# Hybrid attention block: x of the second half scaled by its token norm once, on arrival, and the products with rbc and rcol left out

## Chip, cores and metric

One core of a Trainium2 chip. The metric is the device time of one execution in microseconds, the median of several runs. Engines: TensorE (PE, with its weight loads PEld), VectorE (DVE), ScalarE (ACT), GpSimd (POOL); SyncE (SP) issues most transfers.

## What is computed

A decoder block on x of 1024 tokens by 1024 features: an RMS norm, one projection into eleven parts, latent attention with 8 heads (MLA), gated linear attention with 4 heads (GLA), gates, an output projection, the residual and a final norm. Cut to what matters here:

```python
h = rmsnorm(x, g_in)                       # x * rsqrt(mean(x*x) + EPS) * g_in
proj = h @ w_in
(c_q, c_kv, k_r, z_mla, q_g, k_g, v_g, a_lr, z_gla, gate_mla, gate_gla) = split(proj)
q  = rmsnorm(c_q, g_q) @ w_uq              # latent attention: queries
kv = rmsnorm(c_kv, g_kv) @ w_ukv           # keys and values
y_mla = (mla_attention(q, k, v) * silu(z_mla)) @ w_proj_mla
log_a = log_sigmoid(a_lr @ w_gla_gate + b_gla_gate) / 16
y_gla = (rmsnorm(gla_chunked(q_g, k_g, v_g, log_a), g_gla) * silu(z_gla)) @ w_proj_gla
merged = sigmoid(gate_mla) * y_mla + sigmoid(gate_gla) * y_gla
out = rmsnorm(x + merged @ w_out, g_final)
```

The norm's factor is one number per token (r below). Since it multiplies a whole row of x, it may be applied to x or to each product x @ w.

## The kernel before

The tokens are worked in two halves of 512, h = 0 and h = 1, one after the other. Activations lie transposed, features on partitions and the 512 tokens along the row. Each fp32 product is made of three: both operands are split into a rounded high part and a low part (`split`, line 209: ACT copies to the high part, DVE or POOL subtracts for the low part), and `mm3` (line 191, matmuls at line 201) adds high x high, high x low and low x high in PSUM. Weights are fetched by SP (`load_raw`), split by ACT (`whi`, line 187) and DVE or POOL (`wlo`, line 188).

The work is a list of units per half (`units_of`): misc, the latents ckv and cq, per GLA head q, k, v and two z units, 16 gate units g, then the attention's units (uqr, uv, hi, zm), yg, ym and the output units wo. A `Stream` steps through them in order, a few matmuls at a time, and fills the waits of the side chains (`st.ride`, `tick`). A scheduler then orders each engine's instructions; every engine works its own list strictly in that order.

`prologue(h)` (line 266) fetches x for a half: four tiles transposed (`xs`, two k tiles of 128 features each), scaled by g_in alone and split into xh and xl (lines 281, 282), and four tiles by rows (`xr`), whose squares ACT sums (line 289) to ssq; `rsqrt_cols` makes rcol, r with tokens on partitions, 128 x 4. `bcast_row` (line 254) later spreads it over the partitions: four small matmuls (line 257) and a copy by ACT (line 259) give rbc, 128 x 512. For h = 1 the prologue runs among the output units of half 0 (`pro`, at the end), in pools with 3 buffers.

So x @ w still lacks r, and every user of a projection puts it in: `silu2` and the gate units multiply by rbc on DVE (lines 337, 349) ahead of ACT's tanh; the q units multiply both decay factors ep (DVE, 373) and en (POOL, 374); the values are scaled by rcol while they are split (409, 410); krr = misc x rbc (663); `latent` carries rcol in its row sums (f1, f2, f3). The 16 gate results go through DRAM (`gtd`) and are fetched again into `zr` at the end of the half; the linear branch's results come back the same way in `linear_inputs` (`ugd`), before whose last fetch all gate units must be done (line 988).

## Time and profile before

| | |
|---|---|
| median of 3 runs | 1083.74 us (1082.48 to 1083.81) |
| profiled execution | 1085.81 us, of which the span from first to last instruction is 1084.0 |
| PE busy | 1048.3 us, 97% of the span |
| DVE busy | 714.0 us, 66% |
| ACT busy | 542.1 us, 50% |
| POOL busy | 374.9 us, 35% |
| mean granted clock of PE | 0.98 |
| half 1 begins on PE | 517.81 us |

Times in the trace count from the first instruction. A row of a timeline gives start, duration, engine, line, operation, output <- inputs, shapes and count, and in brackets how long the engine had been idle and what ended that. Matmuls overlap, so a row's duration is longer than the step from one to the next. The chain of waits is followed back from the last instruction, at each step to whatever released it.

### The profile page before, as it was taken

What the parts mean: (1) busy time and instruction counts of PE and PEld (TensorE: products, weight loads), DVE (VectorE), ACT (ScalarE), POOL (GpSimd) and SP (SyncE); (2) the same over time, 40 slices, a digit from 0 to 9 for tenths busy, and PEclk for the clock granted to TensorE, in tenths of its full rate; (3) what the DMA queues carried; (4) which work ended last, traced back from release to release, by engine and by line L of the source; (5) the groups of instructions that cost most, each with busy time, mean ns of one, the idle gap of its engine ahead of it and who ended that gap; (6) DMA issues with size and microseconds to landing.
All of it is one profiled execution on the core that took longest, in us unless ns stands there. A gap on an engine that the chain in (4) does not pass through costs nothing.

```text
span 1084.0 us, 14078 instructions
## 1 busy us (share of the span) xinstructions
PE 1048.3 (97%) x5231; PEld 872.4 (80%) x5231; DVE 714.0 (66%) x1114; ACT 542.1 (50%) x910; POOL 374.9 (35%) x274
## 2 busy tenths in 40 slices
PE   8999999999999989999999999999999998999997
PEld 5798998987778867888889989988777776788875
DVE  5796555557586776466887655455767877667673
ACT  5744334455556653444574444344664656553232
POOL 2361121114445542230524211104454656533420
PEclk8899999999999999999999999999999999899999
DMA  8213213235433446644412233235422223424532
GB/s 297 98 59 97 97 60 117 97 100 195 139 98 111 144 139 250 226 138 144 165 60 78 78 102 101 80 112 158 122 96 70 81 83 121 125 90 161 175 111 98
DMA packets 46118, 132.05 MB, mean 122 GB/s; under 512 B 5232, under 2 KB 7664, under 8 KB 45920
## 3 DMA queue, kind: packets, MB, share of 16 engines
q1 hardware_dynamic: 37760, 113.96, 32.1%
q0 software_dynamic: 3680, 8.78, 3.0%
q10 hardware_dynamic: 4608, 8.39, 2.1%
q8 instruction: 41, 0.67, 0.3%
q14 instruction: 29, 0.24, 0.1%
HBM read 110.01 MB, written 21.10 MB: 121 GB/s over the span
## 4 chain that ended last, share of the span: by engine, by line
PE 77%; DVE 12%; ACT 4%; issue 2%; DMA 2%; POOL 1%; SPq 0%; POOLq 0%; DVEq 0%; ACTq 0%
PE pj L201 58%; DVE pl L943 2%; PE y L548 2%; PE y L546 2%; PE y L547 2%; PE ops L201 2%; DVE mx L893 1%; PE sc L930 1%; PE sc L932 1%; PE sc L933 1%; PE ov L951 1%; PE ov L952 1%; PE sc L886 1%; PE at L201 1%; DVE wlo L188 1%
## 5 line engine op out<-in xcount | busy, mean ns | idle before, releaser
L201 PE MATMUL pj<-xl,whi 128*128 128x512 f32 x800 | 301.0, 399 | 1.4 <-DVE xl L282 1.4
L201 PE MATMUL pj<-xh,whi 128*128 128x512 f32 x672 | 270.5, 403 | 2.4 <-ACT whi L187 1.6
L187 ACT CAST whi<-wraw 128x1024 fp32r<-128x1024 f32 (+1 forms) x151 | 155.3, 1029 | 122.0 <-PE pj L201 91.3
L201 PEld LDWEIGHTS pj<-xl,whi 128*128 128x128 f32 x800 | 153.5, 192 | 31.9 <-DVE xl L282 2.9
L201 PE MATMUL pj<-xh,wlo 128*128 128x512 f32 x672 | 176.6, 397 | 0.0
L188 POOL TENSOR_TENSOR wlo<-wraw,whi 128x1024 fp32r<-128x1024 f32 (+2 forms) x52 | 118.2, 2274 | 140.8 <-ACT whi L187 67.4
L201 PEld LDWEIGHTS pj<-xh,whi 128*128 128x128 f32 x672 | 129.7, 193 | 28.0 <-ACT whi L187 1.9
L201 PEld LDWEIGHTS pj<-xh,wlo 128*128 128x128 f32 x672 | 127.2, 191 | 26.3
L188 DVE TENSOR_TENSOR wlo<-wraw,whi 128x1024 fp32r<-128x1024 f32 x100 | 127.4, 1275 | 21.5 <-ACT whi L187 21.3
L945 POOL TENSOR_TENSOR acc<-acc,p 128x512 f32<-128x512 f32 (+3 forms) x80 | 84.9, 1061 | 86.0 <-ACT p L939 70.5
L943 DVE TENSOR_TENSOR pl<-p,ph 128x512 fp32r<-128x512 f32 (+3 forms) x80 | 70.3, 886 | 23.4 <-ACT ph L942 23.2
L939 ACT ACTIVATE p<-sc 128x512 f32<-128x512 f32 (+3 forms) x80 | 37.3, 468 | 68.8 <-DVE sc L935 50.8
L201 PE MATMUL pj<-wlo,xh 128*128 128x256 f32 x256 | 64.4, 285 | 0.0
L201 PE MATMUL pj<-whi,xh 128*128 128x256 f32 x256 | 64.2, 284 | 0.0
L893 DVE TENSOR_REDUCE mx<-sc 128x1 f32<-128x512 f32 (+2 forms) x96 | 51.8, 551 | 11.6 <-PE sc L886 10.4
L548 PE MATMUL y<-whi,zl 128*128 128x512 f32 x128 | 50.5, 396 | 0.5 <-DVE zl L211 0.5
L547 PE MATMUL y<-wlo,zh 128*128 128x512 f32 x128 | 50.4, 395 | 0.0
L546 PE MATMUL y<-whi,zh 128*128 128x512 f32 x128 | 49.5, 396 | 0.0
L201 PEld LDWEIGHTS pj<-wlo,xh 128*128 128x128 f32 x256 | 49.0, 191 | 0.3
L201 PEld LDWEIGHTS pj<-whi,xh 128*128 128x128 f32 x256 | 48.9, 191 | 0.3
L211 POOL TENSOR_TENSOR ql<-qi,qh 128x512 fp32r<-128x512 f32 x8 | 12.4, 1554 | 93.5 <-ACT qh L210 93.5
L349 DVE TENSOR_TENSOR zr<-pj,rbc 128x512 f32<-128x512 f32 x32 | 22.0, 688 | 33.8 <-PE pj L201 33.5
(298 smaller groups left out, 2101.6 us busy)
## 6 DMA issues: line engine op xcount, KB each, us to landing
wraw<-in_dram SPq DMA_DIRECT2D x141, 512.0 KB, 3.5
gtd<-zr ACTq DMA_DIRECT2D x32, 256.0 KB, 2.2
zr<-gtd SPq DMA_DIRECT2D x32, 256.0 KB, 2.9
xr<-in_dram SPq DMA_DIRECT2D x8, 512.0 KB, 9.4
ugd<-uo SPq DMA_DIRECT2D x16, 256.0 KB, 2.2
zr<-ugd SPq DMA_DIRECT2D x16, 256.0 KB, 3.1
xo<-in_dram SPq DMA_DIRECT2D x8, 512.0 KB, 5.8
xs<-in_dram SPq DMA_DIRECT2D x7, 512.0 KB, 8.6
```

The costliest lines, as they stand in the source:

```text
L187: nc.scalar.copy(out=hi[:, 0:n], in_=raw[:, 0:n])
L188: getattr(nc, lo_engine).tensor_tensor(out=lo[:, 0:n], in0=raw[:, 0:n], in1=R(hi[:, 0:n]), op=ALU.subtract)
L201: nc.tensor.matmul(out=ps, lhsT=a, rhs=b, start=(i == 0), stop=(i == 3 * n - 1))
L211: (lo_engine or nc.vector).tensor_tensor(out=lo, in0=src, in1=R(hi), op=ALU.subtract)
L349: nc.vector.tensor_tensor(out=zr, in0=c.ps, in1=c.rbc, op=ALU.mult)
L546: nc.tensor.matmul(out=c.ops[t], lhsT=a[0], rhs=b[0], start=(k == 0), stop=False)
L547: nc.tensor.matmul(out=c.ops[t], lhsT=a[0], rhs=b[1], start=False, stop=False)
L548: nc.tensor.matmul(out=c.ops[t], lhsT=a[1], rhs=b[0], start=False, stop=(k == 7))
L893: nc.vector.reduce_max(mx[:, t, b:b + 1], ps[:, 0:n], axis=mybir.AxisListType.X)
L939: nc.scalar.activation(p[:, 0:n], ps[:, 0:n], AF.Exp, scale=SCALE)
L943: nc.vector.tensor_tensor(out=pl[:, 0:n], in0=p[:, 0:n], in1=R(ph[:, 0:n]), op=ALU.subtract)
L945: nc.gpsimd.tensor_tensor(out=s.acc[:, q0:TH], in0=s.acc[:, q0:TH], in1=p[:, 0:n], op=ALU.add)
```

## The change

Half 0 stays as it is. For half 1 a new `prologue1` fetches the row tiles first, makes rcol, spreads it at once (PSUM tile `y`, among the output units of half 0), and multiplies each transposed tile by g_in and rbc on DVE before it is split. Every user in half 1 then works without r: the gate units' tanh and `silu2` read the projection in PSUM, ep and en stay as they are, the values are split plainly, krr is a copy by ACT, `latent` loses f1 and two small products. The last fetch of `linear_inputs` no longer waits for gate unit 15 in half 1.

```diff
+    def prologue1(pl, bufs, fps):
+        c = hv[1]
+        ssq = mk(up, [P, 4], F32, "ssq")
+        for t in range(4):
+            xr = mk(pl, [P, D], F32, "xr", bufs=bufs)
+            nc.sync.dma_start(out=xr, in_=x[1, t])
+            nc.scalar.activation(xr, xr, AF.Square, accum_out=ssq[:, t:t + 1])
+            yield
+        rcol = mk(up, [P, 4], F32, "rcol")
+        rsqrt_cols(rcol, ssq, 1.0 / D)
+        c.xh = mk(xgp, [P, KT, TH], F32R, "xh")
+        c.xl = mk(xgp, [P, KT, TH], F32R, "xl")
+        yield
+        rbc = mk(up, [P, TH], F32, "rbc")
+        bcast_row(rcol, rbc, mk(fps, [P, TH], F32, "y"))
+        for kp in range(4):
+            rv = mk(pl, [P, 2, TH], F32, "xs", bufs=bufs)
+            nc.sync.dma_start(out=rv, in_=xt[1, kp])
+            for a in range(2):
+                kt = 2 * kp + a
+                nc.vector.scalar_tensor_tensor(out=rv[:, a, :], in0=rv[:, a, :], scalar=vcol(V_GIN, kt), in1=rbc,
+                                               op0=ALU.mult, op1=ALU.mult)
+                split(c.xh[:, kt, :], c.xl[:, kt, :], rv[:, a, :])
+            yield
...
         def silu2(ps):
-            zr = mk(up, [P, TH], F32, "zr", bufs=2)
-            nc.vector.tensor_tensor(out=zr, in0=ps, in1=c.rbc, op=ALU.mult)
+            zr = ps
+            if h == 0:
+                zr = mk(up, [P, TH], F32, "zr", bufs=2)
+                nc.vector.tensor_tensor(out=zr, in0=ps, in1=c.rbc, op=ALU.mult)
...
                 zr = mk(up, [P, TH], F32, "zr", bufs=2)
-                nc.vector.tensor_tensor(out=zr, in0=c.ps, in1=c.rbc, op=ALU.mult)
-                nc.scalar.activation(zr, zr, AF.Tanh, scale=0.5)
+                if h == 0:
+                    nc.vector.tensor_tensor(out=zr, in0=c.ps, in1=c.rbc, op=ALU.mult)
+                nc.scalar.activation(zr, zr if h == 0 else c.ps, AF.Tanh, scale=0.5)
...
-                nc.vector.tensor_tensor(out=ep, in0=ep, in1=c.rbc, op=ALU.mult)
-                nc.gpsimd.tensor_tensor(out=en, in0=en, in1=c.rbc, op=ALU.mult)
+                if h == 0:
+                    nc.vector.tensor_tensor(out=ep, in0=ep, in1=c.rbc, op=ALU.mult)
+                    nc.gpsimd.tensor_tensor(out=en, in0=en, in1=c.rbc, op=ALU.mult)
...
+                        if h == 1:
+                            split(vh[:, t, :], vl[:, t, :], ps[:, a, :])
+                            continue
...
-            bps = mk(gps, [P, TH], F32, "tr")
-            bcast_row(c.rcol, c.rbc, bps)
-            nc.vector.tensor_tensor(out=krr, in0=c.misc, in1=c.rbc, op=ALU.mult)
+            if h == 0:
+                bps = mk(gps, [P, TH], F32, "tr")
+                bcast_row(c.rcol, c.rbc, bps)
+                nc.vector.tensor_tensor(out=krr, in0=c.misc, in1=c.rbc, op=ALU.mult)
+            else:
+                nc.scalar.copy(out=krr, in_=c.misc)
...
+                else:
+                    nc.vector.tensor_copy(out=f2.unsqueeze(2), in_=sums)
                 rsqrt_cols(f3, f2, 1.0 / width)
-                nc.vector.tensor_tensor(out=f3, in0=f3, in1=c.rcol, op=ALU.mult)
+                if h == 0:
+                    nc.vector.tensor_tensor(out=f3, in0=f3, in1=c.rcol, op=ALU.mult)
...
+                    if f == 7 and h == 0:
+                        st.upto(f"{h}g15")
                     if f == 7:
-                        st.upto(f"{h}g15")
                         slots.append(mk(up, [P, TH], F32R, "rbc"))
...
-                pro = prologue(1, fp, 3)
+                pro = prologue1(fp, 3, fps)
```

The order of the instructions follows from the code and the scheduler. Three places show what moves (the line numbers of the change are its own).

ACT at the start of half 1, before: `csq` and `crawcq` are the square and the copy of a query latent's projection, `ep` the first decay factor.

```order
L187 CAST whi<-wraw 128x1024
L370 ACT_TABLE_LOAD
L370 ACTIVATE ep<-rel 128x512
L326 ACTIVATE csq<-pj 128x512
L327 COPY crawcq<-pj 128x512
L372 ACTIVATE en<-rel 128x512
```

The same place of the change:

```order
L187 CAST whi<-wraw 128x1024
L352 ACTIVATE csq<-pj 128x512
L353 COPY crawcq<-pj 128x512
L210 CAST chik<-crawckv 128x512 x2
L399 ACT_TABLE_LOAD
L399 ACTIVATE ep<-rel 128x512
L401 ACTIVATE en<-rel 128x512
```

The last square and copy now stand ahead of ep. On PE the row sums of these squares (`at<-one,csq`) stood as two, three large matmuls, then ten, and stand now as twelve in one piece, 18 large matmuls after the latent's last one; each is two rows of a timeline.

DVE at the end of half 0, the change: `xs` is a transposed tile of x, `xl` its low part, `xo` the output with its residual, `y` the output projection.

```order
L188 TENSOR_TENSOR wlo<-wraw,whi 128x1024
L317 SCALAR_TENSOR_TENSOR xs<-xs,vecs,rbc 128x512 x6
L211 TENSOR_TENSOR xl<-xs,xh 128x512 x2
L188 TENSOR_TENSOR wlo<-wraw,whi 128x1024
L211 TENSOR_TENSOR xl<-xs,xh 128x512 x2
L586 SCALAR_TENSOR_TENSOR xo_4423<-y,xo_4423 128x512
L211 TENSOR_TENSOR xl<-xs,xh 128x512 x2
L586 SCALAR_TENSOR_TENSOR xo_4424<-y,xo_4424 128x512
L317 SCALAR_TENSOR_TENSOR xs<-xs,vecs,rbc 128x512 x2
```

Before, the same stretch held the two weight pieces and the residual sums alone; all eight xl were made ahead of the first residual sums. The broadcast's matmuls stand on PE 60 matmuls ahead of half 1's first one.

DVE in the attention of half 1, where the row maxima of the fifth head end, before: `mt` is the row maximum, `pl` the low part of the exponentials, `zr` a gate unit's product with rbc.

```order
L901 TENSOR_SCALAR mt<-m_8139 128x4
L902 SCALAR_TENSOR_TENSOR mt<-m_8139,mt 128x4
L943 TENSOR_TENSOR pl<-p,ph 128x384
L349 TENSOR_TENSOR zr<-pj,rbc 128x512
L935 TENSOR_TENSOR sc<-sc,msk 128x128 x2
L943 TENSOR_TENSOR pl<-p,ph 128x256
```

And the change:

```order
L941 TENSOR_SCALAR mt<-m_8099 128x4
L942 SCALAR_TENSOR_TENSOR mt<-m_8099,mt 128x4
L983 TENSOR_TENSOR pl<-p,ph 128x384
L975 TENSOR_TENSOR sc<-sc,msk 128x128 x2
L983 TENSOR_TENSOR pl<-p,ph 128x256
```

The product is gone; ACT's tanh reads the projection itself. The same holds for all 15 gated and gate units of this stage.

## Rows read from the trace of the kernel before

**Rows 1.** The page: busy time of engines, and the chain's shares by engine.
```profile
PE 1048.3 (97%) x5231; PEld 872.4 (80%) x5231; DVE 714.0 (66%) x1114; ACT 542.1 (50%) x910; POOL 374.9 (35%) x274
...
PE 77%; DVE 12%; ACT 4%; issue 2%; DMA 2%; POOL 1%; SPq 0%; POOLq 0%; DVEq 0%; ACTq 0%
```

**Rows 2.** Stretches: us, busy of PE, PEld, DVE, ACT, POOL, clock, DMA share, GB/s.
```profile
560.00:572.00 12.00, 10.97 (x45) 8.91 (x45) 11.69 (x21) 5.54 (x11) 7.52 (x5) 0.72 0.16 51
572.00:760.00 188.00, 186.67 (x1116) 165.72 (x1115) 110.65 (x174) 83.04 (x156) 40.53 (x29) 1.00 0.32 102
760.00:920.00 160.00, 150.14 (x673) 118.45 (x672) 122.10 (x202) 94.53 (x159) 90.99 (x66) 0.99 0.32 96
920.00:990.00 70.00, 67.94 (x302) 55.25 (x303) 49.81 (x86) 38.91 (x70) 34.11 (x28) 0.95 0.34 102
```

**Rows 3.** Timeline of PE, start of half 1: start, us, what, [idle before, releaser].
```profile
561.98 2.73 PE L715 MATMUL at<-one,csq 128*128 128x2 f32 x20 [1.03 <-ACT csq L326]
```

**Rows 4.** Timeline of ACT, the same stretch.
```profile
560.81 0.63 ACT L370 ACTIVATE ep<-rel 128x512 f32<-128x512 f32 x1 [4.12 <-DVE rel L361]
561.35 0.58 ACT L326 ACTIVATE csq<-pj 128x512 f32<-128x512 f32 x1
```

**Rows 5.** Busy time by stretch, columns as in rows 2: where the clock fell.
```profile
62.13:65.53 3.40, 3.40 (x10) 2.62 (x9) 3.40 (x6) 0.21 (x2) 2.71 (x2) 0.50 0.27 108
563.89:570.70 6.81, 6.81 (x20) 5.46 (x20) 6.50 (x11) 2.47 (x6) 5.70 (x5) 0.50 0.24 79
830.13:833.53 3.40, 3.40 (x10) 2.84 (x9) 1.22 (x6) 2.93 (x7) 1.19 (x2) 0.50 0.45 151
922.29:929.10 6.81, 5.57 (x14) 4.44 (x15) 5.24 (x10) 3.67 (x7) 5.89 (x6) 0.50 0.65 189
```

**Rows 6.** Timeline of PE, the same place in half 0.
```profile
59.11 2.73 PE L715 MATMUL at<-one,csq 128*128 128x2 f32 x24
```

**Rows 7.** Timeline of PE, end of half 0 and start of half 1.
```profile
517.81 0.40 PE L201 MATMUL pj<-xh,whi 128*128 128x512 f32 x1
518.04 0.40 PE L201 MATMUL pj<-xl,whi 128*128 128x512 f32 x1
...
526.01 1.05 PE L257 MATMUL tr<-idn,rcol 128*128 128x128 f32 x8
```

**Rows 8.** Timeline of DVE, end of half 0.
```profile
503.94 1.23 DVE L188 TENSOR_TENSOR wlo<-wraw,whi 128x1024 fp32r<-128x1024 f32 x1 [2.27 <-ACT whi L187]
```

**Rows 9.** Timelines of SP and ACT, half 0: the last x tile.
```profile
485.70 0.33 SPq L278 DMA_DIRECT2D xs<-in_dram  x1
...
489.17 0.72 ACT L281 ACTIVATE xh<-xs,vecs 128x512 fp32r<-128x512 f32 x1 [0.92 <-DMA xs<-in_dram]
```

**Rows 10.** Timeline of POOL, end of half 0.
```profile
511.40 0.56 POOL L568 TENSOR_TENSOR fr<-fr,mhalf 128x1 f32<-128x1 f32 x1 [28.45 <-DVE fr L566]
```

**Rows 11.** Groups of DVE, 483 to 520 us: busy us, mean ns, idle before.
```profile
L282 DVE SCALAR_TENSOR_TENSOR xl<-xs,vecs,xh 128x512 fp32r<-128x512 f32 x8 | 5.6, 746 | 0.3 <-ACT xh L281 0.3
```

**Rows 12.** Groups of DVE, attention of half 1, 765 to 990 us.
```profile
L349 DVE TENSOR_TENSOR zr<-pj,rbc 128x512 f32<-128x512 f32 x11 | 7.5, 684 | 4.7 <-PE pj L201 4.6
L340 DVE SCALAR_TENSOR_TENSOR sz<-sz,onec,zr 128x512 f32<-128x512 f32 x4 | 5.8, 1447 | 0.0
...
L515 DVE SCALAR_TENSOR_TENSOR xh<-zr,onec,pj 128x512 f32<-128x512 f32 x4 | 3.0, 745 | 2.6 <-PE pj L201 2.6
L337 DVE TENSOR_TENSOR zr<-pj,rbc 128x512 f32<-128x512 f32 x4 | 2.7, 686 | 0.5 <-PE pj L201 0.5
```

**Rows 13.** Waits, 765 to 990 us: us in total, times, longest.
```profile
ACT zr L350 <- DVE zr L349: 12.0, 7, 3.6
```

**Rows 14.** Chain of waits, attention of half 1: start, us, what.
```profile
773.08 0.69 DVE zr L337
...
848.11 1.41 DVE sz L340
...
922.00 0.60 DVE zr L349
```

More of the change, by code (lines that the diff above doesn't have):

```diff
@@ L716, in latent @@
                                          start=(i == 0), stop=(i == n - 1))
-                f1 = mk(pp, [P, 4], F32, "f1" + tag)
-                nc.vector.tensor_tensor(out=f1, in0=c.rcol, in1=c.rcol, op=ALU.mult)
+                sums = cps[:, 0:8].rearrange("p (a b) -> p a b", b=2)[:, :, 0:1]
                 f2 = mk(pp, [P, 4], F32, "f2" + tag)
-                nc.vector.tensor_tensor(out=f2.unsqueeze(2), in0=cps[:, 0:8].rearrange("p (a b) -> p a b", b=2)[:, :, 0:1],
-                                        in1=f1.unsqueeze(2), op=ALU.mult)
                 f3 = mk(pp, [P, 4], F32, "f3" + tag)
+                if h == 0:
+                    f1 = mk(pp, [P, 4], F32, "f1" + tag)
+                    nc.vector.tensor_tensor(out=f1, in0=c.rcol, in1=c.rcol, op=ALU.mult)
+                    nc.vector.tensor_tensor(out=f2.unsqueeze(2), in0=sums, in1=f1.unsqueeze(2), op=ALU.mult)
+                else:
+                    nc.vector.tensor_copy(out=f2.unsqueeze(2), in_=sums)
                 rsqrt_cols(f3, f2, 1.0 / width)
-                nc.vector.tensor_tensor(out=f3, in0=f3, in1=c.rcol, op=ALU.mult)
+                if h == 0:
+                    nc.vector.tensor_tensor(out=f3, in0=f3, in1=c.rcol, op=ALU.mult)
                 yield 3
```

## Prediction

> **What bounds the kernel now.** I read the page first, then busy time by stretch, then the timelines of the stretches in which TensorE (PE) loses time, and last the groups, waits and chain there. On the page PE is busy 97% of the span and holds 77% of the chain, DVE 12% [rows 1]. So a DVE instruction that is taken away gives back time only where PE waits for DVE, or for something queued behind DVE. The stretches say where that is in half 1: in the GLA part PE is busy 186.67 of 188.00 us, while in the attention it misses 9.9 of 160 and 2.1 of 70 us, and around 560 us it misses 1.0 of 12 at a mean clock of 0.72 [rows 2]. What the change removes in the GLA part is therefore worth nothing. That concerns most of the scaled copies of values, all eight products of decay and rbc, and 8 of the 12 gated units: PE runs there at full pace with them. What counts is the start of half 1, its attention, and the seam between the halves, where the new work lies.
>
> The start first. At 561.98 PE idled 1.03 us for csq, the square of the last query latent [rows 3]. ACT had been free for 4.12 us, but its next instruction in order was ep, which waited for DVE's rel; csq stood behind it and ran at 561.35 [rows 4]. From 563.89 to 570.70 the granted clock was then 0.50, the lower level (1.2 GHz instead of 2.4), for 20 matmuls [rows 5].
>
> **The change, part by part.**
>
> *Start of half 1.* The order printed above puts both csq and its copy ahead of ep in ACT's queue. csq then waits for its own matmuls alone, and the 18 large matmuls between them and the reduction (18 x 0.23 = 4.1 us [rows 7]) cover ACT's 0.58 us [rows 4]. Saved: 1.0 us. What is late next is the reduction's own result: f3q is wanted by PE 25 matmuls (5.7 us) after it, and DVE reaches f2q without the product ep x rbc before it; I cost this at nothing. Is the clock's fall saved too? In half 0 the same 24 tiny matmuls ran for 2.73 us from 59.11 with no wait ahead of them [rows 6], and the clock fell all the same, for 3.40 us from 62.13 [rows 5]. The new order has just that pattern: two large matmuls, the 24 tiny ones, six large ones. So I let one stretch of 3.40 us stay in place of 6.81. At half speed a stretch costs half its length: 3.4 becomes 1.7, saved 1.7. Bounds: 0 (the fall stays as it is) and 3.4. The Trainium skill, "TensorE: Matmul & The Clock Gate", section "Part 1: The HAM clock gate", says that idleness throttles the clock and that activity releases it. By that alone the fall would go with the wait, and the start would give 4.4 instead of 2.7; the row of half 0, a fall without a wait, speaks for the smaller value, which I take.
>
> *Attention of half 1.* Eleven gate units and four gated ones lose their product with rbc on DVE: 11 x 0.684 + 4 x 0.686 = 10.3 us, and 5.1 us in which DVE stood waiting for their matmuls [rows 12]. In the chain of waits such pieces stand five times, 0.60 to 0.69 us each, 3.25 us in all (the first and the last stand in [rows 14]). That is what lies on the path; the rest runs beside PE. The four gated units also end in a product sz x zr that now reads PSUM instead of a second SBUF tile. It took 1.447 us on average; the nearest row with an operand in PSUM and the same operation took 0.745 [rows 12]. On the chain the four pieces hold 5.05 us (one: 1.41 [rows 14]), against 4 x 0.745 = 2.98: 2.1 us less. No row shows this operation itself from PSUM, so it is bounded by 0 and 2.1; I take half, 1.05. Attention together: 4.3 us, bounds 0 (another wait was close behind each time) and 5.3. ACT's tanh now waits for the matmuls itself, where it waited for DVE (7 times, 12.0 us [rows 13]): behind it stand the exponentials of the scores, then as now, and it starts one DVE product earlier. I cost that at nothing; it is the slower rival below.
>
> *The seam.* What is added: eight products x g rbc on DVE, a split of each k tile into a plain copy and a plain difference in place of a scaled copy and a scaled difference, a broadcast of rcol on PE and its copy on ACT. The same eight fetches of x stand in SP's queue, the row-wise ones first now, with the same bytes ahead of each gate fetch: nothing. The broadcast's matmuls took 1.05 us at 526.01 [rows 7]; they move from half 1 into the output stage, nothing in sum. They now stand 60 matmuls before the first one of half 1, so at 517.81 - 60 x 0.23 = 504.0 us [rows 7]; with the matmuls and a copy like csq's of 0.58 [rows 4] rbc is there at 505.6, when DVE is just through with the weight piece of 503.94 [rows 8]. From then DVE has 16 instructions of 0.75 us (the present xl: 0.746 [rows 11]), one weight piece of 1.23 [rows 8] and the residual sums among them. Six products end at 510.1, two xl at 511.6, the weight piece at 512.8, two more xl at 514.3, and xl five and six, behind one residual sum of some 0.7, at 516.5. PE, now 1.05 later, wants the first pair at 518.9 and a pair every 0.46 us [rows 7]: six pairs are ready. The last two come from the fourth fetch of x, which waits for the first tile's buffer (511.6) behind six weight loads in SP's queue. The same fetch came 3.5 us after its issue before (485.70 to 489.17 [rows 9]); now it lands near 515, its products end near 518.7 and the copies and differences by 522.5. The order lets PE take matmuls of the next unit meanwhile: the seventh xh stands at place 13 (521.6), the last xl in the forties (528). POOL, which could slow DVE, was idle for 28.45 us until 511.40 [rows 10]. So I cost the seam at nothing, with 0 and 5.2 (below) as bounds. krr comes some 1.5 us later, since PE mixes the first unit with the second; its next user, the decay matmuls, moved from place 70 to 77 (1.6 us), which covers it.
>
> *Small parts together.* krr becomes a copy on ACT, f1 and two 128x4 products go, the last fetch for the linear branch no longer forces the sixteenth gate first: nothing on the path.
>
> **The sum.** 1.0 + 1.7 + 4.3 = 7.0 us. Against the profiled execution of 1085.81 us (span 1084.0) that is 1078.8. The median of the runs, 1083.74, is 2.07 below that execution, so the prediction is 1076.7. Its own range is 1073 to 1080. A measurement can tell about 0.2% (2.2 us) from no change.
>
> **The rivals.**
>
> *The clock stays up.* With the wait gone the start's fall goes wholly, 1083.74 - 4.4 - 4.3 = 1075.0; if the two falls in the attention (3.40 and 6.81 us [rows 5], up to 5.1 us) go with the DVE waits before them and sz is saved in full, 1069. Against it speaks half 0's fall. The page named above stands on this side. Chance 0.15.
>
> *The attention gains nothing.* Each DVE piece on the chain had another wait just behind it (scores, exponential, DMA of gates), since PE alone holds 77% of the chain and its other suppliers are never far; only the start counts: 1083.74 - 2.7 = 1081.0. Chance 0.17.
>
> *x is late at the seam.* Its instructions all read two SBUF tiles, and one with two SBUF inputs took 1.447 in the attention against 0.745 [rows 12], with POOL running beside it. Were they all so long, 16 x 0.7 = 11.2 us more, of which 8.4 fall before the sixth xl: 516.5 becomes 524.9, wanted at place 12, 518.9 + 11 x 0.23 = 521.4. That is 3.5 us of waiting and a half-clock stretch after it, 1.7: 1076.7 + 5.2 = 1081.9. POOL's idle time speaks against it [rows 10]. The Trainium skill, "SBUF — State Buffer", section "SBUF: two separate sides", has DVE and GpSimd lock each other out in such instructions; here it would act only if POOL had work there. Chance 0.08.
>
> *Slower: the wait moves into ACT's queue.* The place is the fifteen tanh of the attention. DVE used to absorb the wait for a unit's last matmul; now ACT does, with the exponential of the scores behind it, which DVE and then PE await. If each tanh holds ACT for the mean of 1.7 us (12.0 / 7 [rows 13]), that is 25.7 us, 13.7 more than now; a third of it on the path, as 5 of 15 products were, is 4.6, and nothing is gained there: 1083.74 - 2.7 + 4.6 = 1085.6. With waits nearer the longest, 3.6 [rows 13], 1088 and more. It decides from about 14 us of new waiting on ACT. For it: ACT's queue is strict, as the wait at 560.81 shows [rows 4]. Against: a tanh that needs no DVE product starts earlier. Chance 0.10, at 1088.
>
> That the change fails to do what it says is no rival: the order shows the products gone from DVE.
>
> **How the numbers follow.** Forecast 0.50, clock 0.15, nothing in the attention 0.17, seam 0.08, ACT 0.10. Faster by over 0.2% is under 1081.6: forecast and clock in full and half of the case at 1081.0, 0.50 + 0.15 + 0.085, rounded to 0.74; within 0.2% its other half and the seam, 0.085 + 0.08, rounded to 0.16; slower 0.10. The range runs from the full clock case, 1069, to 1085, which takes in the cases near 1081 with a miss of 3 us and leaves out the slower rival and the edges of the others.
>
> **What would show it.** Right: no PE idling for csq near 560 us, and a half-clock stretch of 3.4 us or none there; no DVE line of products with rbc in half 1; sz near 0.75 us; PE in the attention missing some 4 us less; no PE wait on xh or xl at the seam. Wrong: PE waiting for xl near 520 us, exponentials waiting on tanh in ACT's queue, or an attention as long as before.

## The result, and the profile after

The changed kernel took 1069.65 us (median of 6 runs, 1069.03 to 1073.22) beside 1082.01 us for the kernel before on the same chip (1080.93 to 1083.81): a ratio of 0.9892, 95% interval 0.9873 to 0.9910, or 11.7 us of some 1082 with 9.7 to 13.7 as bounds. The forecast was 7.0 us less. The side was right, but the size was too small by two fifths: the time lies outside 1073 to 1080, which the prediction gives as its own range, and inside the wider range of 1069 to 1085 by only 0.65 us.

The profiled execution took 1069.29 us with a span of 1067.5. The profiled execution of before lay 2 to 4 us above its own medians, so a difference of the two traces (16.5 us) overstates the gain; the traces are therefore read stage by stage, and the ratios decide.

The page of the changed kernel answers to [rows 1]. DVE lost 30.9 us of busy time, PE 8.8, though it runs just as many matmuls.

```profile
PE 1039.5 (97%) x5231; PEld 867.5 (81%) x5231; DVE 683.1 (64%) x1085; ACT 539.4 (51%) x911; POOL 375.0 (35%) x270
...
PE 73%; DVE 14%; ACT 5%; DMA 4%; issue 3%; POOL 2%; SPq 0%; POOLq 0%; DVEq 0%; ACTq 0%
```

**The start of half 1.** The timeline of PE answers to [rows 3], the timeline of ACT to [rows 4], the busy time by stretch to the second of [rows 5].

```profile
556.75 2.73 PE L751 MATMUL at<-one,csq 128*128 128x2 f32 x24
...
566.18 1.16 PE L257 MATMUL tr<-idn,f3q 128*128 128x128 f32 x8 [0.86 <-POOL f3q L252]
```

```profile
552.97 0.62 ACT L352 ACTIVATE csq<-pj 128x512 f32<-128x512 f32 x1
553.46 0.61 ACT L353 COPY crawcq<-pj 128x512 f32<-128x512 f32 x1
```

```profile
553.60:565.60 12.00, 11.72 (x64) 9.79 (x62) 11.62 (x21) 5.49 (x9) 4.42 (x3) 1.00 0.26 88
565.60:745.00 179.40, 178.82 (x1081) 159.61 (x1082) 91.56 (x152) 78.43 (x152) 34.07 (x26) 1.00 0.31 101
```

The square is done 3 us before PE wants it, all 24 tiny matmuls stand together, and the clock stayed at its upper level. A wait of 0.86 us for the reduction's own result (f3q) is new. From the first matmul of half 1 to the first transpose of ki the two traces need 68.3 us before and 63.5 after; 1.05 of the difference is the broadcast, which moved to the output stage. Behind that the linear part runs as before, at full pace.

**The attention of half 1.** Its whole length, from the first score to the first matmul of the output, in the kernel before and then in the changed one (busy time by stretch, columns as in [rows 2]), and the one half-clock stretch that is left of the two in [rows 5]:

```profile
767.50:1023.40 255.90, 243.99 (x1088) 194.60 (x1087) 186.91 (x298) 136.55 (x232) 134.02 (x101) 0.98 0.37 113
```

```profile
761.40:1006.80 245.40, 239.61 (x1088) 192.66 (x1087) 173.41 (x284) 135.84 (x232) 137.94 (x101) 0.99 0.38 119
906.70:910.11 3.41, 3.41 (x10) 2.71 (x9) 2.51 (x5) 1.66 (x4) 3.41 (x2) 0.50 0.69 223
```

10.5 us less for the same 1088 matmuls. Of these, 6.1 are time in which PE stood (11.9 before, 5.8 now), and 4.4 are busy time, most of it the clock: 10.2 us at the lower level before, 3.4 now, and half of that difference is 3.4 us.

The groups of DVE there answer to [rows 12], the waits of ACT to [rows 13] (us in total, times, longest):

```profile
L368 DVE SCALAR_TENSOR_TENSOR sz<-sz,onec,pj 128x512 f32<-128x512 f32 x4 | 3.0, 740 | 0.1
```

```profile
ACT zr L379 <- PE pj L201: 3.0, 3, 1.7
...
ACT sz L367 <- PE pj L201: 1.1, 2, 0.7
```

The last product of the gated units takes 0.740 us from PSUM, 1.447 before. ACT's fifteen tanh wait 4.1 us for matmuls (gate units 3.0, gated units 1.1); the slower rival needed 25.7.

**The seam.** Groups of DVE, 495 to 530 us, answer to [rows 11]:

```profile
L211 DVE TENSOR_TENSOR xl<-xs,xh 128x512 fp32r<-128x512 f32 x8 | 7.4, 960 | 0.0
L317 DVE SCALAR_TENSOR_TENSOR xs<-xs,vecs,rbc 128x512 f32<-128x512 f32 x8 | 5.5, 746 | 2.0 <-ACT rbc L259 2.0
```

The eight products take 0.746 us each, as the row of before had it. PE waits for nothing between 512 and 545 us.

### The profile page after: what moved, and what is told of

Read it like the earlier page. It is cut to its first block, busy times and chain, and to the rows that moved or that the text cites. A ratio compares the mean times of both kernels' runs of the same rounds, so it can differ in the third digit from the quotient of the medians.

```text
span 1067.5 us, 14030 instructions
## 1 busy us (share of the span) xinstructions
PE 1039.5 (97%) x5231; PEld 867.5 (81%) x5231; DVE 683.1 (64%) x1085; ACT 539.4 (51%) x911; POOL 375.0 (35%) x270
## 4 chain that ended last, share of the span: by engine, by line
PE 73%; DVE 14%; ACT 5%; DMA 4%; issue 3%; POOL 2%; SPq 0%; POOLq 0%; DVEq 0%; ACTq 0%
PE pj L201 55%; PE ops L201 2%; DVE wlo L188 2%; DMA zr<-gtd 2%; PE sc L970 1%; PE y L580 1%; PE sc L972 1%; PE y L581 1%; DVE pl L983 1%; PE sc L973 1%; PE ov L992 1%; PE y L579 1%; PE ov L991 1%; PE sc L926 1%; DVE mx L933 1%
## 5 line engine op out<-in xcount | busy, mean ns | idle before, releaser
L201 PE MATMUL pj<-xl,whi 128*128 128x512 f32 x800 | 297.6, 395 | 0.6 <-DVE xl L282 0.6
L201 PE MATMUL pj<-xh,whi 128*128 128x512 f32 x672 | 267.3, 399 | 1.2 <-ACT whi L187 0.8
L562 POOL TENSOR_TENSOR zr<-zr,xh 128x512 f32<-128x512 f32 x16 | 27.6, 1742 | 45.7 <-DVE zr L561 45.7
```

The costliest lines, as they stand in the source:

```text
L201: nc.tensor.matmul(out=ps, lhsT=a, rhs=b, start=(i == 0), stop=(i == 3 * n - 1))
L562: nc.gpsimd.tensor_tensor(out=t2, in0=t2, in1=c.m2[:, j, :], op=ALU.add)
```

## The experiments

Ratios are to the kernel before, run beside each on the same chip; 0.001 is 1.08 us. What is put back "by ones" multiplies by a column of ones, so that only the cost returns.

### Which part of the attention holds the gain

The pieces were put back one by one and together.

```diff
# f1_fence
-                    if f == 7 and h == 0:
+                    if f == 7:
                         st.upto(f"{h}g15")
# f2_gate
-                if h == 0:
-                    nc.vector.tensor_tensor(out=zr, in0=c.ps, in1=c.rbc, op=ALU.mult)
-                nc.scalar.activation(zr, zr if h == 0 else c.ps, AF.Tanh, scale=0.5)
+                nc.vector.tensor_tensor(out=zr, in0=c.ps, in1=c.rbc if h == 0 else onec.broadcast_to([P, TH]), op=ALU.mult)
+                nc.scalar.activation(zr, zr, AF.Tanh, scale=0.5)
# f3_silu: the same in silu2, into a zr tile; f4_all: f1, f2 and f3 together
```

Fence:

> The changed kernel with one thing put back: before the last fetch of the linear branch in half 1 all sixteen gate units must again be done. Theory fence (the seven us that one head of the attention, the one around 908 to 940 us, lost less come from this fence): that head is some 32 us long again and the time is 1075 to 1077 us, 0.995 of before. Theory products (the gain comes from DVE's products with rbc and what queued behind them): no change, 1069.7 us, 0.989 of before, and that head stays near 25 us. Theory order (any edit there shuffles the schedule by a few us): 1067 to 1073 with heads that changed where no fence is.

Gate units:

> The changed kernel with the gate units' product put back on DVE in half 1, by a column of ones instead of rbc, ahead of the tanh. Theory products: eleven products of 0.68 us come back in the attention and DVE stands again for their matmuls; two thirds of the gain of the attention beyond the gated units' part, 4 to 6 us, is lost: 1074 to 1076 us. Theory of the prediction (only the pieces on the chain of before count): 11 of 15 of 3.25, 2.4 us: 1072 us. Theory fence: nothing, 1069.7 us.

Gated units:

> The changed kernel with the gated units' product put back in half 1, by a column of ones; they take a zr buffer again, and their last product reads two SBUF tiles. Theory of the prediction: 4 of 15 of 3.25 and the 1.05 of the last product, 1.9 us: 1071.6 us. Theory buffers (the zr buffers, two in all, are what held the fetches of the linear branch and ACT behind them in the head at 908 to 940): that head is long again, 5 to 7 us: 1075 to 1077 us. Theory fence: nothing, 1069.7 us.

All three:

> The changed kernel with all three put back at once: fence, the gate units' product and the gated units' product, by ones. Its attention is that of before, its start of half 1 and its seam are the new ones. If the attention's part of the gain is what the traces say, 10 us, it runs at 1079 to 1080 us, 0.998 of before, and only the start is left, 2 to 4 us. By the terms of the prediction (attention 4.3 us) it would be 1074 us. If the gain lies in the order alone, anything between 1070 and 1080 with the long head in another place.

Measured: fence 0.9872 (0.9853 to 0.9891), gate units 0.9928 (0.9909 to 0.9948), gated units 0.9960 (0.9946 to 0.9973), all three 0.9965 (0.9951 to 0.9979).

- The fence costs nothing. With it the head from 903 to 934 us, taken from one row sum on PE to the next, is 31.2 us long instead of 24.4, just as the theory of the fence said, yet the kernel is no slower: the head holds matmuls of other units that come later otherwise. The trace alone had put 7 us of the gain into that one head, and that was wrong. Lengths of heads don't add up to a gain where filler moves between them.
- All three together leave 0.9965: start and seam are worth 3.8 us (2.3 to 5.3), and the attention the rest, 0.0073 or 7.9 us (5.3 to 10.5).
- Products of either kind alone bring back much of it: those of the gate units (eleven in the attention) 3.9 us, half of it, those of the gated units (four there) 7.4, nearly all. The sum of 11.3 against 7.9 suggests that they use the same slack, but the difference, 3.4 us, is no larger than its interval (3.6 either way).

In the trace of f4_all the attention differs from the changed kernel's as before's did (busy time by stretch): 8.6 us more, 5.5 of them in which PE stood, and 6.8 us at the lower clock in place of 3.4.

```profile
761.30:1015.30 254.00, 242.74 (x1089) 193.34 (x1089) 188.64 (x298) 136.07 (x232) 134.37 (x101) 0.99 0.36 114
913.60:920.40 6.80, 5.89 (x16) 4.14 (x15) 5.25 (x11) 3.81 (x8) 5.89 (x5) 0.50 0.50 155
```

### What a gated unit's product costs by

Written to zr, it adds three things: DVE's time, a zr buffer, and a last product on two SBUF tiles. g1_inplace keeps the first alone, g2_ownbuf the first and third; h1 takes the second and third out of the kernel before; k1 does so in half 0 of the changed kernel.

```diff
# g1_inplace, in silu2
             zr = ps
             if h == 0:
...
+            else:
+                nc.vector.tensor_tensor(out=ps, in0=ps, in1=onec.broadcast_to([P, TH]), op=ALU.mult)
# g2_ownbuf, in place of the lines of zr in silu2
+            zr = mk(up, [P, TH], F32, "zr", bufs=2) if h == 0 else mk(up, [P, TH], F32, "rbc")
+            nc.vector.tensor_tensor(out=zr, in0=ps, in1=c.rbc if h == 0 else onec.broadcast_to([P, TH]), op=ALU.mult)
# h1_before_inplace, in the kernel before
-            zr = mk(up, [P, TH], F32, "zr", bufs=2)
+            zr = mk(up, [P, TH], F32, "zr", bufs=2) if h == 0 else ps
# k1_half0: zr = ps in half 0 as well, multiplied by rbc in place
```

> The changed kernel with the gated units' product put back in half 1, written over the projection in PSUM by ones: DVE has the four products of 0.68 us again and the tanh waits for them, but no zr buffer is taken and the last product still reads PSUM (0.74 us). With a zr tile for it the time had been 1076.85, 0.996 of before. Theory product (DVE's own time and place in its queue ahead of the tanh): most of that loss stays, 1074 to 1077 us, 0.995. Theory second operand (what costs is the last product on two SBUF tiles, 1.0 to 2.2 us instead of 0.74) or theory zr buffers: the gain stays, 1068 to 1070 us, 0.988 to 0.990.

> The changed kernel with the gated units' product put back in half 1, by ones, into a tile of its own (that of rbc, free by then): product, and last product on two SBUF tiles, as in the run with zr at 0.996 of before, but the two zr buffers are left to the gates and the fetches. Theory zr buffers: the gain stays, 0.988 to 0.990. Theory product or second operand: 0.994 to 0.997. With the run in PSUM beside it the three are told apart.

> The kernel before with one edit: in half 1 the gated units' product with rbc is written over the projection in PSUM instead of into a zr tile; everything else, DVE's fifteen products too, as before. Theory second operand or zr buffers: it is faster by a good part of what the gated units are worth in the changed kernel, 3 to 7 us, 0.994 to 0.997 of before. Theory product: no change, 0.999 to 1.001.

> The changed kernel, and in half 0 too the gated units' product is written over the projection in PSUM (rbc is still multiplied there). Theory second operand: half 0's attention, in which four gated units stand as well, gains as half 1's does, at its smaller loss of PE time 1 to 3 us: 0.986 to 0.988 of before. Theory product: nothing, 0.989. Against it: projections stay longer in the three PSUM buffers, which in the linear part of half 0 could cost PE some waits, up to 1 us.

Measured: g1 0.9927 (0.9909 to 0.9945), g2 0.9956 (0.9936 to 0.9976), h1 0.9980 (0.9970 to 0.9991), k1 0.9886 (0.9864 to 0.9907).

A buffer of its own changes nothing that can be measured (0.9956 beside 0.9960), which speaks against the zr buffers. The product alone costs about half of what f3 lost, 3.8 us for 2.7 us of DVE; the second SBUF operand most of the rest, 3.1 us between g1 and g2 (0.2 to 6.0), 2.2 in the kernel before (1.0 to 3.2). That last run fell between the ranges that were expected of either theory. In half 0 no gain shows; the interval leaves room for the 1 to 3 us that were expected there.

Two groups of DVE from 762 to 990 us tell the two costs apart, first in the changed kernel, then in g1_inplace, then in f3_silu; the row of sz in the changed kernel stands above (3.0 us), and that of g1 is 3.0 us as well:

```profile
L983 DVE TENSOR_TENSOR pl<-p,ph 128x512 fp32r<-128x512 f32 x32 | 37.3, 1169 | 9.4 <-ACT ph L982 9.4
```

```profile
L985 DVE TENSOR_TENSOR pl<-p,ph 128x512 fp32r<-128x512 f32 x32 | 42.9, 1344 | 7.9 <-ACT ph L984 7.9
```

```profile
L981 DVE TENSOR_TENSOR pl<-p,ph 128x512 fp32r<-128x512 f32 x32 | 42.9, 1343 | 7.6 <-ACT ph L980 7.6
...
L366 DVE SCALAR_TENSOR_TENSOR sz<-sz,onec,zr 128x512 f32<-128x512 f32 x4 | 6.1, 1514 | 0.0
```

The product makes pl 5.6 us longer in sum. The second operand makes sz itself 3.1 us longer and leaves pl where the product had put it.

Why does 0.69 us on DVE cost more than itself? The timelines of DVE in the two kernels run alike, 0.90 us apart, up to 808 us; then first the changed kernel:

```profile
808.58 0.75 DVE L368 SCALAR_TENSOR_TENSOR sz<-sz,onec,pj 128x512 f32<-128x512 f32 x1
...
810.24 0.86 DVE L983 TENSOR_TENSOR pl<-p,ph 128x512 fp32r<-128x512 f32 x1
...
812.07 0.74 DVE L983 TENSOR_TENSOR pl<-p,ph 128x512 fp32r<-128x512 f32 x1 [0.63 <-ACT ph L982]
...
819.48 1.53 DVE L942 SCALAR_TENSOR_TENSOR mt<-m,mt 128x4 fp32r<-128x4 f32 x1
```

The same stretch with the product (g1_inplace), and two instructions of POOL beside it:

```profile
809.10 0.69 DVE L367 TENSOR_TENSOR pj<-pj,onec 128x512 f32<-128x512 f32 x1
...
811.63 1.61 DVE L985 TENSOR_TENSOR pl<-p,ph 128x512 fp32r<-128x512 f32 x1
...
813.50 1.58 DVE L985 TENSOR_TENSOR pl<-p,ph 128x512 fp32r<-128x512 f32 x1
...
821.58 1.45 DVE L944 SCALAR_TENSOR_TENSOR mt<-m,mt 128x4 fp32r<-128x4 f32 x1
```

```profile
811.40 1.29 POOL L987 TENSOR_TENSOR acc<-acc,p 128x512 f32<-128x512 f32 x1
...
821.48 1.52 POOL L188 TENSOR_TENSOR wlo<-wraw,whi 128x640 fp32r<-128x640 f32 x1
```

The product pushes two pl, differences of two SBUF tiles, under POOL's work, where each takes 1.6 us instead of 0.74 to 0.86. Even the tiny 128x4 step mt ends only when POOL's instruction does, in both kernels. The Trainium skill, "SBUF — State Buffer", section "SBUF: two separate sides", calls the port pair that the two engines share an exclusive lock: a DVE instruction with two SBUF inputs and a GpSimd one that reads SBUF take turns, each for its whole length. The trace agrees: the product that reads PSUM keeps its 0.69 us beside POOL, while pl and mt wait. The prediction used that rule at the seam alone, where POOL was idle. DVE's lateness shows as PE's wait at the row maxima of the next head (mt). PE's waits, first in the changed kernel, then with the product:

```profile
PE sc L947 <- DVE mt L942: 2.3, 3, 1.1
```

```profile
PE sc L949 <- DVE mt L944: 5.1, 4, 1.9
```

### POOL's part, and DVE's

```diff
# n1_after_nosum, n2_all_nosum
-                if kt > 0:
+                if kt > 0 and h == 0:
                     nc.gpsimd.tensor_tensor(out=s.acc[:, q0:TH], in0=s.acc[:, q0:TH], in1=p[:, 0:n], op=ALU.add)
...
+            if h == 1:
+                nc.vector.tensor_scalar(out=ri, in0=rs[0:16], scalar1=1.0, scalar2=1.0, op0=ALU.mult, op1=ALU.add)
...
# q2_wlo
-                gate_unit(next(gates), "gpsimd")
+                gate_unit(next(gates), "gpsimd" if h == 0 else "vector")
```

n1 and n2 leave POOL's sums of the exponentials out of half 1; the small DVE step keeps the reciprocal finite.

> The changed kernel without POOL's sums of the exponentials in half 1: the 56 additions to acc are left out, so the softmax's denominator holds the first key tile alone, plus one (a 16x512 addition on DVE keeps it finite). It serves as the base for the run beside it. In the changed kernel DVE's pl on 512 columns takes 1.17 us on average and 0.69 when POOL is idle. Theory POOL (a DVE instruction on two SBUF tiles runs at half pace while POOL works, and that is what makes DVE late): pl falls below 0.95 us and the time to 1060 to 1066 us, 0.980 to 0.986 of before. Theory queue alone: pl may be shorter, but 0.987 to 0.990.

> The kernel with the attention's products and fence put back (0.9965 of before), also without POOL's 56 additions in half 1. With the additions the products cost 8.5 us against the changed kernel. Theory POOL (a product of 0.69 us pushes later two-tile instructions under POOL's work, where they take up to 1.6 us): without POOL's additions the two kernels come together, a difference of 2 to 5 us. Theory queue alone (DVE is simply late by its own work and waits): the difference stays 7 to 9 us.

> The changed kernel with the weight splits (wlo) of the eleven gate units of half 1's attention moved from POOL (2.4 us each) to DVE (1.2 us or more). Theory POOL: POOL's 26 us less let DVE's two-tile instructions run faster, which pays for part of the 13 to 17 us that DVE gets: 1067 to 1073 us, 0.987 to 0.992. Theory queue alone: DVE's added work costs as the fifteen products did (10.3 us of them cost 8.5), so 10 us or more: 1078 to 1082 us, 0.997 to 1.001. A gain over the changed kernel would be 0.985 or less.

Measured: n1 0.9831 (0.9817 to 0.9846), n2 0.9894 (0.9879 to 0.9909), q2 0.9965 (0.9952 to 0.9979).

Without the sums the changed kernel is another 6.6 us faster, and pl falls from 1.17 to 0.83 us:

```profile
L983 DVE TENSOR_TENSOR pl<-p,ph 128x512 fp32r<-128x512 f32 x32 | 26.3, 826 | 5.9 <-ACT ph L982 5.9
```

The waits at the row maxima all but vanish in both kernels (n1, then n2):

```profile
PE sc L947 <- DVE mt L942: 0.2, 1, 0.2
```

```profile
PE rs L1005 <- ACT ah L210: 0.9, 1, 0.9
...
PE sc L944 <- DVE mt L939: 0.5, 1, 0.5
```

Yet the two stay 6.8 us apart (4.5 to 9.1), against 7.9 with the sums: within the intervals the same. So POOL stretches the lateness that PE pays at the row maxima, but the products cost nearly as much without it; the 2 to 5 us that were expected if POOL were the cause are not wholly ruled out. In n2 much of the cost stands in one place, behind ACT:

```profile
901.19 0.62 ACT L210 CAST chiq<-zr 128x512 fp32r<-128x512 f32 x1 [2.30 <-DMA zr<-ugd]
```

```profile
904.40:914.60 10.20, 9.20 (x20) 6.21 (x21) 8.31 (x15) 7.31 (x13) 3.07 (x4) 0.50 0.51 168
```

ACT waits 2.30 us for a fetch of the linear branch, PE then stands for pl and the row sums (rs), and its clock falls for 10.2 us. Over the attention PE is busy 4.6 us longer than in n1, which has no fall there at all, and stands 2.1 us longer. q2 lost 7.9 us: from 755 to 980 us DVE's weight splits rose from 8 (12.6 us) to 17 (24.7 us), pl took 1.31 us, and POOL's relief did not pay for it.

### Buffers, from two sides

```diff
# r1_all_fetchbuf (from f4_all), r2_after_fetchbuf (from the changed kernel)
-                    ur = mk(up, [P, TH], F32, "zr", bufs=2)
+                    ur = mk(up, [P, TH], F32, "rbc") if h == 1 and f % 2 == 0 else mk(up, [P, TH], F32, "zr", bufs=2)
# m1_gate_inplace (from the changed kernel); h2_before_both: the same in h1, with rbc
-                zr = mk(up, [P, TH], F32, "zr", bufs=2)
                 if h == 0:
...
+                else:
+                    nc.vector.tensor_tensor(out=c.ps, in0=c.ps, in1=onec.broadcast_to([P, TH]), op=ALU.mult)
+                    zr = mk(up, [P, TH], F32, "zr", bufs=2)
                 nc.scalar.activation(zr, zr if h == 0 else c.ps, AF.Tanh, scale=0.5)
```

> The kernel with the attention's products and fence put back (0.9965 of before), and every second fetch of the linear branch in half 1 in a tile of its own (that of rbc) instead of a zr buffer. Theory buffers (the fetches wait for zr, ACT for the fetches): ACT's waits on them near 900 to 925 us go, and with them the stall and the clock's fall there: 3 to 5 us better, 0.992 to 0.994 of before. Theory product: no change, 0.996 to 0.997.

> The changed kernel with the gate units' product put back by ones, but written over the projection in PSUM, so that a zr buffer is taken only for the tanh, as in the changed kernel. With the product written to zr it was 0.9928, against 0.987 to 0.989 without it. Theory buffers: nearly all of that comes back, 0.988 to 0.990. Theory product (eleven times 0.68 us of DVE): it stays, 0.992 to 0.994.

> The kernel before with both products with rbc in half 1 written over the projection in PSUM, gated units and gate units. With the gated units' alone it was 0.998. Theory buffers: the head at 908 to 940 us loses its stall and clock fall, 3 to 4 us more, 0.994 to 0.995. Theory product: 0.998 as with the gated units' alone, since all fifteen products are still there.

> The changed kernel with every second fetch of the linear branch in half 1 in the tile of rbc instead of a zr buffer. Left there are a stall of 1.6 us at 905 to 906 us and one clock fall of 3.4 us behind it, 1.6 us. Theory buffers: up to 3 us better than the changed kernel, 0.985 to 0.987 of before. Theory product or queue: no change, 0.987 to 0.990.

Measured: r1 0.9969 (0.9957 to 0.9982), m1 0.9928 (0.9909 to 0.9948), h2 0.9970 (0.9958 to 0.9981), r2 0.9912 (0.9890 to 0.9933). All four speak against the buffers: r1 stands where f4_all stood, m1 exactly where f2_gate stood, h2 at the edge of h1's interval, and r2 is no faster than the changed kernel but slower by 2.2 us (2.8 either way). The wait for the fetch in n2 is where lateness surfaced, not its source.

### DVE, or any step?

```diff
# c1_gate_act (from m1); c2_silu_act: the same in g1, on ps
-                    nc.vector.tensor_tensor(out=c.ps, in0=c.ps, in1=onec.broadcast_to([P, TH]), op=ALU.mult)
+                    nc.scalar.copy(out=c.ps, in_=c.ps)
```

> The changed kernel with an extra step for the eleven gate units of half 1's attention (and the five before it): the projection is copied onto itself in PSUM by ACT (some 0.6 us) ahead of the tanh. With a product by ones of 0.69 us on DVE at the same place it was 0.9928 of before, without a step 0.987 to 0.989. Theory DVE (its time and its queue): ACT is half idle there, so most of the loss goes, 0.988 to 0.990. Theory step (PSUM buffer held longer, tanh later): the loss stays, 0.992 to 0.994.

> The same for the gated units: an extra copy in PSUM by ACT ahead of the tanh instead of the product by ones on DVE, with which it was 0.9927. Theory DVE: 0.987 to 0.990. Theory step: 0.992 to 0.994.

Measured: c1 0.9923 (0.9906 to 0.9940), c2 0.9922 (0.9909 to 0.9935). The step costs as much on ACT as on DVE as far as the intervals tell (0.0026 either way between c1 and m1, 0.0022 between c2 and g1), so DVE's own time on the product is not what counts. In c2 the wait at the row maxima is that of g1, though DVE has no instruction more than in the changed kernel:

```profile
PE sc L949 <- DVE mt L944: 5.4, 4, 2.0
```

Its ACT ran the copy at 808.20 and the tanh behind it, so the exponential of the next score started at 809.30 and, in DVE's queue, sz at 809.84; a later pl then met POOL and took 1.95 us:

```profile
808.20 0.57 ACT L367 COPY pj<-pj 128x512 f32<-128x512 f32 x1 [0.39 <-PE pj L201]
...
809.30 0.59 ACT L981 ACTIVATE p<-sc 128x512 f32<-128x512 f32 x1
```

```profile
812.97 1.95 DVE L985 TENSOR_TENSOR pl<-p,ph 128x512 fp32r<-128x512 f32 x1
```

The scores pass through both queues in turn (exponential on ACT, pl on DVE), and a step in either delays what is behind it in both: pl takes 42.9 us in c2 from 762 to 990 us, just as in g1. The gate units don't show this: pl takes 36.5 us in m1 and 39.7 in c1, and the wait at the row maxima 2.9 us in each, against 2.3 in the changed kernel. That the projection's PSUM buffer is held longer isn't it: no list of PE's waits in the attention names a matmul into pj. Each edit also shifts the scheduler's order of the instructions behind it; how much of each difference is that order, these runs don't separate. The five edits that add one step to one kind of unit (f2, m1, c1, g1, c2) lie close together, 0.9922 to 0.9928, but the edits that add none spread as well: f1 0.9872, k1 0.9886, r2 0.9912. In the traces, single executions, the stretch from the first score to the first matmul of the output is 245.4 us in the changed kernel, 246.1 in k1 and 247.5 in f1; with a step it is 247.5 in c1, 248.9 in m1, 249.8 in f2, 250.1 in c2 and 250.4 in g1. Yet r2, which only moves fetches to another buffer, needs 250.7, with 4.2 us of PE's waits at the row maxima. So a loss of 3 to 4 us by one kind of step is not cleanly told from a change of order; the 7.4 and 7.9 us of f3 and f4 are.

### The start of half 1 alone

```diff
# b3_csq, in the kernel before
-                nc.scalar.activation(sq[:, i, :], c.ps, AF.Square)
-                nc.scalar.copy(out=raw[:, i, :], in_=c.ps)
+                if h == 1 and tag == "cq" and i == 2:
+                    nc.vector.tensor_copy(out=raw[:, i, :], in_=c.ps)
+                    nc.vector.tensor_tensor(out=sq[:, i, :], in0=raw[:, i, :], in1=c.ps, op=ALU.mult)
+                else:
+                    nc.scalar.activation(sq[:, i, :], c.ps, AF.Square)
+                    nc.scalar.copy(out=raw[:, i, :], in_=c.ps)
```

> The kernel before with one edit: at the start of half 1 the copy and the square of the last query latent are made by DVE, not by ACT, where the square stood behind ep. Nothing else of the change is in it. If the start's gain is the wait for csq and the clock's fall behind it, PE does not wait there and 2.5 to 4.4 us are gained: 0.996 to 0.998 of before. By the terms of the prediction 2.7 us, 0.9975. If that gain lay in the broadcast or in the products that are gone, 0.999 to 1.001; DVE's own queue there could also make the square late, and then the wait stays.

Measured: 1.0048 (1.0036 to 1.0060), 5.2 us slower. The edit moved the wait instead of removing it: on DVE the square stood behind a weight piece and ep x rbc, ran at 565.32, and PE waited 3.12 us, with 10.2 us at the lower clock.

```profile
566.04 4.43 PE L719 MATMUL at<-one,csq 128*128 128x2 f32 x20 [3.12 <-DVE csq L328]
```

```profile
565.10:575.30 10.20, 9.26 (x33) 8.29 (x34) 5.94 (x14) 2.40 (x4) 2.54 (x2) 0.50 0.25 95
```

As a test of the start alone it failed; as a dose it shows that a longer wait for csq is paid in full and more. What the start is worth comes from f4_all.

No version beat the changed kernel by more than the intervals: f1 and k1 stand level with it, and n1 leaves work out.

## Why the prediction fell short, and where it held

*Start of half 1, 2.7 us: the side and nearly the size, the clock's share by luck.* Measured with the seam, 3.8 (2.3 to 5.3). csq ahead of ep took the wait away (1.0), as forecast. "I cost this at nothing", said of f3q, failed by 0.6 to 0.94 us where the clock stayed up. "So I let one stretch of 3.40 us stay" was a coin (below): no fall in the profiled execution, one in eight of the 15 variants. And "At half speed a stretch costs half its length" doesn't hold here: from the first matmul of half 1 to the first transpose of ki h1_before_inplace, with the wait and without a fall, needs 66.7 us, the kernel before and h2_before_both, with the wait and the same fall, 68.3, so the whole fall of 6.81 us cost 1.6 and not 3.4. Of the 4.8 us down to the changed kernel's 63.5 that leaves 3.2, of which 1.05 is the moved broadcast and 2.2 the new order.

*Seam, 0: right.* rbc came at 503.2 us (forecast 505.6), the six products ended at 507.3 (510.1), and no matmul waited. What the rival feared showed only after half 1 had begun: beside two weight pieces of POOL (516.30 to 521.66 us) an xo took 2.23 us and the last xl 2.89, and PE didn't need them yet.

*GLA part and small parts, 0: right.* The linear part between the start and the attention took 181.4 us before and 181.5 after.

*Attention, 4.3 us with 5.3 as upper bound: mis-sized.* Measured 7.9 (5.3 to 10.5). The step that failed is "That is what lies on the path; the rest runs beside PE". I counted a product as worth its own duration, and only where it stood in the chain: five pieces, 3.25 us. The runs show instead that the four products of the gated units alone cost 3.8 us for 2.7 us of DVE (g1), and that a step of 0.6 us on ACT at the same place costs as much (c2): it shifts the queue of the scores behind it, where the chain names pl, mx or mt and not the product. For the gate units the ratios say the same (m1, c1), the traces less clearly. The second part of the term, "I take half, 1.05" for sz, was short as well: g1 against f3 gives 3.6 us (1.2 to 6.0), h1 2.2, and the four sz are 2.8 us shorter together than before (5.8 to 3.0), where the bound from the chain's pieces was 2.1. And the clock's fall behind the attention's stalls, which I gave to a rival alone, took 1.7 (beside f4's trace) to 3.4 us (beside that of before) of it.

*The rivals.* The clock rival named the right sources, at 1075 down to 1069, though a fall of 3.4 us stayed in the attention. That the time landed at its far end is owed in part to the kernel before, which ran 1.7 us faster beside it than in the prediction's base; as ratios the rival's two ends are 0.9919 and 0.9864, and 0.9892 lies between them. "The attention gains nothing" and "x is late at the seam" fall by the ratios and the seam's rows. The slower rival falls by ACT's 4.1 us of waiting for matmuls; its mechanism is real, though: c1 and c2 put a step into ACT's queue and lost over 3 us each.

*What stays open.* Which single instruction turns a late step into PE's stall in each head; how much of a loss of 3 to 4 us is the order alone; and why eleven products of gate units cost no more (3.9 us) than four of gated units (3.8 us, g1), without a longer pl.

## What to carry to other kernels

The pieces of an instruction that stand in the chain of waits do not price its removal, when it sits in an in-order queue through which the critical loop also passes; here they were too small. Put the cost back alone, at its place, and measure, and beside it an edit that changes the order and adds no cost. An engine that is idle half of the time is no free place for a step if the loop runs through its queue. And a longer stretch of one head or tile in a trace is no loss until it is known that no filler work moved into it.

## What the runs showed of the hardware

**The clock at the start of half 1.** In 16 profiles (the changed kernel and its 15 variants) PE runs the same sequence there: 24 tiny matmuls, no wait ahead of them. In eight the clock fell to its lower level 2.2 to 3.1 us after they began, for 3.4 us in seven and 6.8 in one; in the other eight it did not. f2_gate is one of the first kind; the row of PE shows no wait:

```profile
559.47 2.73 PE L750 MATMUL at<-one,csq 128*128 128x2 f32 x24
```

```profile
562.30:565.70 3.40, 3.40 (x9) 2.65 (x9) 3.40 (x5) 3.37 (x5) 3.33 (x2) 0.51 0.08 14
```

Conversely h1_before_inplace has the wait of the kernel before, 1.03 us, and no fall:

```profile
560.80 2.39 PE L715 MATMUL at<-one,csq 128*128 128x2 f32 x20 [1.03 <-ACT csq L326]
```

```profile
557.00:570.00 13.00, 11.19 (x61) 9.04 (x59) 12.69 (x21) 6.16 (x12) 7.05 (x5) 1.00 0.21 75
```

So neither side of the prediction's argument, half 0's pattern or the rule that idleness throttles, tells what happens there in one execution; all profiles have a fall that begins between 58 and 67 us, about the like place of half 0. The fall here was also nearly free: in the eight profiles that have it PE never waits for f3q, in the eight without it waits 0.60 to 0.94 us, and from the first matmul of half 1 to the first transpose of ki the two kinds need 63.9 (the longest fall: 65.5) and 63.2 to 63.6 us.
